# A work tile for each direction of the DeltaNet block inverses, and one decay buffer fewer

## The chip, the cores and the metric

The kernel runs on one core of one Trainium2 chip (trn2). The metric is the device time of one execution in microseconds (us), as the median of several runs. The core has five engines with a queue each: TensorE (PE in the profile, its weight loads PEld), VectorE (DVE), ScalarE (ACT), GpSimd (POOL) and SyncE (SP), which here only issues DMA transfers. Every queue is worked off in the order in which it was written.

## The reference

Two encoder layers on a (1, 1024, 1024) input. Layer 0 mixes tokens by softmax attention, layer 1 by a bidirectional gated DeltaNet; each is followed by a gated MLP with a short convolution. What matters here is the DeltaNet scan. Per direction and per chunk of 64 tokens it needs the inverse of a unit lower triangular matrix:

```
gc = cumsum(g); decay = exp(where(incl, gc[c] - gc[s], -inf))
L = (k*beta) @ k^T * decay * strict
sol = triangular_solve(L + I, [v*beta, k*beta*exp(gc)])      # u, w
attn = q @ k^T * decay
step:  v_new = u - w @ state;  o = q*exp(gc) @ state + attn @ v_new
       state = state*exp(gc_last) + k_dec^T @ v_new
```

The backward direction runs the same on the flipped sequence. There are 16 value heads on 8 key heads.

## The kernel before

All large products are float32 values split into two float32r parts (`split`, L108: an ACT cast to `hi`, a DVE subtraction to `lo`), and three matmuls of 128x512 for each pair of blocks (`dense`, L126, matmul at L134). They are the bulk of PE's work, here called the dense matmuls.

In the DeltaNet stage (`gdn`, L771) a loop runs over eight key heads j. Each pass emits the input projections of the next key head (`gdn_in`, L452: six products of 48 dense matmuls, a five-tap convolution on DVE at L448, silu on ACT at L449, and the results put into a DRAM tensor `pk`), and then, for the directions d = 0 and 1 of head j, `decay`, `inverse` and `chain`, and last `head_out`. A direction holds sixteen 128x128 blocks (eight double chunks, two value heads).

- `decay` (L539) builds the decayed blocks in four groups of four. Each group takes a tile `pr` from a ring of eight buffers, loads rows of cumulated gates into it from DRAM (`grow`, L549, an SP queue DMA), adds bias and mask (L551, DVE), takes exp (L553, ACT), makes `at` (L558), turns `pr` into the decayed q·k block (L559), and splits `at` into two float16 tiles `ah` (L561) and `al` (L562).
- `inverse` (L583) inverts all sixteen blocks together in a float16 tile `t0` and its transpose `w0`. It first clears with POOL those off-diagonal blocks of `t0` that the other direction filled (two memsets at L601, one at L602), writes the 32x32 diagonal blocks from `ah` (L606, DVE), multiplies with a mask into `w0` (L607, DVE), and starts on PE with products with an identity (L593, output `ip`, input `id`). Four levels of doubling follow, each PE to ACT or DVE and back, then the off-diagonal blocks (L640 to L664) and one refinement step (L672 to L681), which reads `t0` and `w0` to the end.
- `chain` (L685) steps through eight chunks. Step t loads `c` from `pk`, and reads the `pr` tile of group t // 2 as weights in its last matmul (L738). A `pr` buffer is free when the second step that uses it has passed L738.

`t0` and `w0` exist once and serve both directions of all heads. The order within each queue is made by a scheduler before the run, from priorities: `decay` and `inverse` are emitted inside `ahead(4)`, `chain` inside `ahead(2)`, so that they go before the dense matmuls of `gdn_in` where they are ready, and the dense matmuls fill what is left. When the last `gdn_in` is through, the output projection begins (L809): `split_rows` loads the finished heads' rows (`t<-od`) and splits them into `base` and `y` tiles, and dense matmuls with them follow. This place is called the seam below.

Of the kernel before, what the change touches and what calls it, by code (L numbers as in the profile page):

```python
# [9 lines left out]
F32 = mybir.dt.float32  # L10
F32R = mybir.dt.float32r
F16 = mybir.dt.float16
# [6 lines left out]
P = 128  # L19
# [18 lines left out]
def flat(t):  # L38
    return t.rearrange("p a b -> p (a b)")


class Trunk:
# [327 lines left out]
    def gates(self, ys, dp, tmp):  # L370


        nc, ap = self.nc, self.ap
# [12 lines left out]
        every = lambda t: t.rearrange("p (j v) -> p j v", v=2).unsqueeze(2).broadcast_to([P, 8, NC, 2])  # L386
        dtb = self.load("dtb", [P, 2, 16], dp, ap["gdn_dt"].partition_broadcast(P))
        alog = self.load("alog", [P, 2, 16], dp, ap["gdn_alog"].partition_broadcast(P))
        tri = dp.tile([P, 4, P], F32, name="pr", bufs=8)[:, :2]
        nc.sync.dma_start(out=tri, in_=ap["tri"])  # L390
        nc.scalar.activation(out=alog, in_=alog, func=AF.Exp)
        nc.vector.tensor_scalar(out=flat(alog), in0=flat(alog), scalar1=-1.0, scalar2=None, op0=ALU.mult)
# [8 lines left out]
        t = [flat(work()) for _ in range(4)]  # L401
# [137 lines left out]
    def decay(self, j, d, kks, qks, dp):  # L539


        nc = self.nc
        ah, al, prs = {}, {}, {}
        for i in (range(4) if d == 0 else range(3, -1, -1)):
            if i // 2 not in ah:
                ah[i // 2], al[i // 2] = (dp.tile([P, 8, P], F16, name=n, bufs=3) for n in ("ah", "al"))
            pr = prs[i] = dp.tile([P, 4, P], F32, name="pr", bufs=8)
            m0 = 16 * j + 4 * i
            nc.sync.dma_start(out=pr, in_=self.grow[d, m0:m0 + 4].partition_broadcast(P))  # L549
            for m in range(4):  # L550
                nc.vector.scalar_tensor_tensor(out=pr[:, m], in0=pr[:, m], in1=self.maskneg[:, d],  # L551
                                               scalar=self.ebias[:, d, m0 + m:m0 + m + 1], op0=ALU.add, op1=ALU.add)
            nc.scalar.activation(out=pr, in_=pr, func=AF.Exp)  # L553
            prn = pr.rearrange("p (n v) c -> p n v c", v=2)
            bc = lambda t: (t[i // 2][:, (i % 2) * 256:(i % 2) * 256 + 256].rearrange("p (n c) -> p n c", n=2)
                            .unsqueeze(2).broadcast_to([P, 2, 2, P]))
            at = dp.tile([P, 4, P], F32, name="at", bufs=1)
            nc.vector.tensor_tensor(out=at.rearrange("p (n v) c -> p n v c", v=2), in0=prn, in1=bc(kks), op=ALU.mult)  # L558
            nc.vector.tensor_tensor(out=prn, in0=prn, in1=bc(qks), op=ALU.mult)  # L559
            hi, lo = (t[i // 2][:, 4 * (i % 2):4 * (i % 2) + 4] for t in (ah, al))  # L560
            nc.scalar.copy(out=hi, in_=at)  # L561
            nc.vector.tensor_tensor(out=lo, in0=at, in1=hi, op=ALU.subtract)  # L562
        return ah, al, prs

    def delta_buffers(self, dp):
        nc = self.nc
        self.t0, self.w0 = (dp.tile([P, 16, P], F16, name=n, bufs=1) for n in ("t0", "w0"))
        nc.gpsimd.memset(self.t0, 0.0)
        self.maskneg = self.load("maskneg", [P, 2, P], dp)
        self.negoff = self.load("negoff", [P, P], dp)  # L570
        self.lvl = self.load("lvl", [P, 2, 4, 32], dp)
        self.cw5 = self.load("gdn_cw", [P, 32, 6], dp)
        self.o_gain = self.load("gdn_gain", [P, 1], dp)
        half = {}
        for n, w in (("mask2", P), ("id32", 32)):
            t = self.load(n, [P, w], dp)
            half[n] = dp.tile([P, w], F16, name=n + "_16", bufs=1)
            nc.vector.tensor_copy(out=half[n], in_=t)
        self.mask2, self.id32 = half["mask2"], half["id32"]
        self.nident16 = dp.tile([P, P], F16, name="nident16", bufs=1)  # L580
        nc.vector.tensor_scalar(out=self.nident16, in0=self.ident, scalar1=-1.0, scalar2=None, op0=ALU.mult)

    def inverse(self, d, ah, al, dp):  # L583
# [1 line left out]


        nc = self.nc
        t0, w0 = self.t0, self.w0
        up = [(Q32[i], Q32[i + 1]) for i in (0, 2)]
        dn = [(Q32[i + 1], Q32[i]) for i in (0, 2)]  # L590
        a, b = (slice(0, 64), slice(64, 128)) if d == 0 else (slice(64, 128), slice(0, 64))
# [5 lines left out]
        small = lambda n: dp.tile([P, 16, 32], F16, name=n, bufs=2 if n == "tp" else 1)  # L597


        for r, c in (up if d == 0 else dn):  # L600
            nc.gpsimd.memset(t0[r, :, c], 0.0)  # L601
        nc.gpsimd.memset(t0[a, :, b], 0.0)  # L602
        for h in ah:
            hs = slice(8 * h, 8 * h + 8)
            for q in Q32:
# [61 lines left out]
        for h in (range(4) if d == 0 else range(3, -1, -1)):  # L667
# [7 lines left out]
            r = dp.tile([P, 4, P], F16, name="r", bufs=2)  # L675
# [716 lines left out]
```

## Time and profile before

| what | value |
| --- | --- |
| median of 3 runs | 3449.74 us (3447.62 to 3450.36) |
| time of the profiled execution | 3439.26 us |
| its span, first to last instruction | 3437.5 us |
| mean granted TensorE clock | 0.981 of full speed |

The profiled execution is a run of its own, with the hardware profiler on. Its span lies 1.8 us below its own time, and its time 10.5 us below the median. Busy times and waits below are from it. A row's "idle before" is time in which the engine had nothing running, with the instruction that ended it; a wait on an engine that isn't the bound costs nothing.

### The profile page before, as it was taken

How to read it: one execution, taken by the hardware profiler on the slowest of the kernel's cores; microseconds unless marked ns; L12 is line 12 of the kernel's file. 1: busy time of each engine (PE TensorE's matmuls, PEld its weight loads, DVE VectorE, ACT ScalarE, POOL GpSimd, SP SyncE). 2: the span in 40 equal slices, each digit the busy share in tenths (PEclk: the TensorE clock that was granted, in tenths of full speed). 3: DMA queues.
4: the chain of work that ended last, by engine and by line, in shares of the span. 5: the costliest groups of instructions: out<-in, count | busy, mean ns of one | idle time of the engine just before them, and what ended most of it. 6: DMA issues, size and time to landing. Idle time of an engine off the chain costs nothing. (4 is left out here: it accounts for less than half of the span.)

```text
span 3437.5 us, 54135 instructions
## 1 busy us (share of the span) xinstructions
PE 3247.3 (94%) x19690; PEld 2620.0 (76%) x19690; DVE 2495.2 (73%) x4235; ACT 1741.5 (51%) x3224; POOL 842.4 (25%) x919
## 2 busy tenths in 40 slices
PE   7999999899999998899999999999898989999998
PEld 6877788677777876677777777777676867777786
DVE  5335886887776875778778787877853787777695
ACT  4235664544454454565555556666532544544453
POOL 1111330444442002121221212222120144444100
PEclk9999999999999999999999999999999999999999
DMA  3331006333324642332342424334356623332743
GB/s 127 104 113 59 32 31 191 122 106 111 112 94 168 218 129 65 102 111 88 113 126 81 136 92 130 102 113 132 102 175 206 204 98 110 101 105 92 244 132 109
DMA packets 249802, 411.20 MB, mean 120 GB/s; under 512 B 25536, under 2 KB 76096, under 8 KB 249536
## 3 DMA queue, kind: packets, MB, share of 16 engines
q1 hardware_dynamic: 249536, 407.76, 36.6%
q8 instruction: 155, 2.54, 0.3%
q14 instruction: 111, 0.91, 0.1%
HBM read 294.80 MB, written 107.61 MB: 117 GB/s over the span
## 5 line engine op out<-in xcount | busy, mean ns | idle before, releaser
L134 PE MATMUL mm<-base,wh 128*128 128x512 f32 x1248 | 480.1, 412 | 10.0 <-ACT base L109 5.9
L109 ACT CAST wh<-w_raw 128x512 fp32r<-128x512 f32 x275 | 169.9, 619 | 296.7 <-PE mm L134 175.6
L110 DVE TENSOR_TENSOR wl<-w_raw,wh 128x512 fp32r<-128x512 f32 x275 | 193.2, 707 | 138.2 <-ACT wh L109 137.1
L134 PE MATMUL mm<-yh,wh 128*128 128x512 f32 x736 | 282.6, 413 | 5.3 <-ACT t L291 2.7
L134 PE MATMUL mm<-yh,wl 128*128 128x512 f32 x736 | 280.6, 410 | 1.0 <-DVE wl L110 1.0
L134 PE MATMUL mm<-yl,wh 128*128 128x512 f32 x736 | 279.3, 408 | 0.3 <-POOL yl L110 0.2
L134 PEld LDWEIGHTS mm<-base,wh 128*128 128x128 f32 x1248 | 238.3, 191 | 49.6 <-ACT base L109 6.3
L153 POOL TENSOR_TENSOR rs<-rs,power 128x8 f32<-128x8 f32 (+2 forms) x38 | 63.8, 1679 | 824.8 <-DVE rs L152 824.7
L134 PE MATMUL mm<-base,wl 128*128 128x512 f32 x624 | 257.3, 412 | 6.4 <-DVE wl L110 6.4
L703 POOL TENSOR_SCALAR kd<-c,yds 128x128 f32<-128x128 f32 x224 | 95.2, 437 | 635.0 <-PE cp L732 444.8
L109 ACT CAST wh<-a 128x512 fp32r<-128x512 f32 x164 | 101.8, 622 | 256.7 <-PE mm L134 122.6
L109 ACT CAST wh<-s 128x512 fp32r<-128x512 f32 x212 | 131.4, 620 | 183.6 <-PE sp L134 87.3
L134 PE MATMUL sp<-base,wh 128*128 128x512 f32 (+1 forms) x672 | 211.5, 372 | 12.6 <-ACT wh L109 12.6
L448 DVE SCALAR_TENSOR_TENSOR t<-mm,gdn_cw,t 128x1023 f32<-128x1023 f32 (+1 forms) x128 | 163.1, 1276 | 6.8 <-ACT t L445 6.1
L134 PEld LDWEIGHTS mm<-yh,wh 128*128 128x128 f32 x736 | 140.6, 193 | 29.3 <-ACT t L291 3.6
L134 PEld LDWEIGHTS mm<-yl,wh 128*128 128x128 f32 x736 | 140.8, 192 | 27.8 <-POOL yl L110 1.6
L134 PEld LDWEIGHTS mm<-yh,wl 128*128 128x128 f32 x736 | 140.8, 191 | 26.5 <-DVE wl L110 1.7
L134 PE MATMUL sp<-base,wl 128*128 128x512 f32 (+1 forms) x432 | 157.7, 365 | 1.4 <-DVE wl L110 0.9
L134 PEld LDWEIGHTS sp<-base,wh 128*128 128x128 f32 x672 | 127.7, 190 | 34.3 <-ACT wh L109 13.0
L110 DVE TENSOR_TENSOR wl<-s,wh 128x512 fp32r<-128x512 f32 x170 | 142.0, 836 | 12.3 <-ACT wh L109 12.2
L978 POOL TENSOR_TENSOR s<-a,a 128x512 f32<-128x512 f32 x80 | 108.5, 1356 | 159.0 <-DVE s L978 106.0
L134 PEld LDWEIGHTS mm<-base,wl 128*128 128x128 f32 x624 | 119.1, 191 | 27.2 <-DVE wl L110 7.2
(522 smaller groups left out, 9362.4 us busy)
## 6 DMA issues: line engine op xcount, KB each, us to landing
a<-in_ffn_up_dram SPq DMA_DIRECT2D x160, 256.0 KB, 2.8
c<-pk SPq DMA_DIRECT2D x128, 320.0 KB, 3.1
w_raw<-in_gdn_in_dram SPq DMA_DIRECT2D x100, 256.0 KB, 2.8
g_t<-t SPq DMA_DIRECT2D x88, 256.0 KB, 2.0
raw<-g_t SPq DMA_DIRECT2D x88, 256.0 KB, 2.6
w_raw<-in_gdn_out_dram SPq DMA_DIRECT2D x68, 256.0 KB, 3.6
g<-t SPq DMA_DIRECT2D x66, 256.0 KB, 2.1
raw<-g SPq DMA_DIRECT2D x66, 256.0 KB, 2.8
```

Of the source, the lines that this page charges most:

```text
L109: self.nc.scalar.copy(out=hi, in_=src)
L110: (engine or self.nc.vector).tensor_tensor(out=lo, in0=src, in1=hi.bitcast(F32), op=ALU.subtract)
L134: self.nc.tensor.matmul(acc if one else acc[:, hs], lhsT=a, rhs=y[:, hs], start=(first and not onto and k + t == 0), stop=(last and k == n ...
L153: nc.gpsimd.tensor_tensor(out=r, in0=v, in1=self.power[:, :w], op=ALU.pow)
L448: nc.vector.scalar_tensor_tensor(out=o, in0=a, scalar=c[:, i:i + 1], in1=o, op0=ALU.mult, op1=ALU.add)
L703: nc.gpsimd.tensor_scalar(out=kd[:, e], in0=kn, scalar1=col(self.yds, e), scalar2=1.0, op0=ALU.mult, op1=ALU.mult)
L978: e.tensor_tensor(out=s[i], in0=x, in1=z, op=op)
```

## The change

`t0` becomes a list of two tiles, one for each direction, both cleared in full at the start. `w0` stays one tile (the list holds it twice). Each inverse clears now the blocks that it itself filled in the head before, in its own tile, since nothing else writes there. The number and sizes of these clears stay as they were; one full memset is added at the start. The ring `pr` has seven buffers in place of eight; its first allocation, `tri` in `gates`, is from the same ring.

```diff
-        tri = dp.tile([P, 4, P], F32, name="pr", bufs=8)[:, :2]
+        tri = dp.tile([P, 4, P], F32, name="pr", bufs=7)[:, :2]
...
-            pr = prs[i] = dp.tile([P, 4, P], F32, name="pr", bufs=8)
+            pr = prs[i] = dp.tile([P, 4, P], F32, name="pr", bufs=7)
...
-        self.t0, self.w0 = (dp.tile([P, 16, P], F16, name=n, bufs=1) for n in ("t0", "w0"))
-        nc.gpsimd.memset(self.t0, 0.0)
+        self.t0 = [dp.tile([P, 16, P], F16, name=f"t{d}", bufs=1) for d in range(2)]
+        self.w0 = 2 * [dp.tile([P, 16, P], F16, name="w0", bufs=1)]
+        for t in self.t0:
+            nc.gpsimd.memset(t, 0.0)
...
-        t0, w0 = self.t0, self.w0
+        t0, w0 = self.t0[d], self.w0[d]
...
-        for r, c in (up if d == 0 else dn):
+        for r, c in (dn if d == 0 else up):
             nc.gpsimd.memset(t0[r, :, c], 0.0)
-        nc.gpsimd.memset(t0[a, :, b], 0.0)
+        nc.gpsimd.memset(t0[b, :, a], 0.0)
```

With eight buffers, each `pr` of a direction takes over the buffer that the same group of the same direction had one head earlier. With seven, the first three groups take over buffers of groups two to four of that direction one head earlier, and the fourth takes over the buffer of the first group of the direction just before it: the inverse of (j, 1) can't be begun in full before the chain of (j, 0) has passed its second step, and that of (j, 0) not before the chain of (j-1, 1) has.

The scheduler puts all queues of the DeltaNet stage in another order; outside of it a few rows of the second MLP move. Three places follow. The lines after the change are three higher from L571 on.

The queue of SP around head 5 (`pk5`), with tile numbers. Before: the last two `pr` loads of (5, 1) stand among the stores of head 5's `v` rows, ahead of the first loads of its chain (`c`).

```order
L549 DMA pr_23433<-grow_11848 128x512
L468 DMA pk5_20202<-h_20651 128x4x128
L549 DMA pr_23445<-grow_11848 128x512
L468 DMA pk5_20202<-h_20659 128x4x128
L121 DMA w_raw_22252<-in_gdn_in_dram 128x512
L121 DMA w_raw_22435<-in_gdn_in_dram 128x512
L121 DMA w_raw_22441<-in_gdn_in_dram 128x512
L468 DMA pk5_20202<-h_20735 128x4x128
L468 DMA pk5_20202<-h_20743 128x4x128
L121 DMA w_raw_22500<-in_gdn_in_dram 128x512
L698 DMA c_23208<-pk5_20202 128x640
L698 DMA c_23225<-pk5_20202 128x640
```

After: the fourth of them (`pr_23447`) stands behind four `c` loads of the chain of (5, 0).

```order
L701 DMA c_23210<-pk5_20204 128x640
L701 DMA c_23227<-pk5_20204 128x640
L771 DMA od8_22097<-z_22124 128x512
L121 DMA w_raw_22508<-in_gdn_in_dram 128x512
L701 DMA c_23254<-pk5_20204 128x640
L766 DMA z_22133<-zd9_18602 128x512
L701 DMA c_23281<-pk5_20204 128x640
L771 DMA od9_22098<-z_22133 128x512
L549 DMA pr_23447<-grow_11850 128x512
```

So this load moved from before the chain of (5, 0) to behind its second step.

The queue of DVE at the same inverse, from the fourth group's first operation to the mask product that ends the preparation. Before:

```order
L551 SCALAR_TENSOR_TENSOR pr<-pr,ebias,maskneg 128x128 x4
L558 TENSOR_TENSOR at<-pr,kks 128x512
L559 TENSOR_TENSOR pr<-pr,qks 128x512
L448 SCALAR_TENSOR_TENSOR t<-mm,gdn_cw,t 128x1022
L562 TENSOR_TENSOR al<-at,ah 128x512
L606 TENSOR_TENSOR t_11705<-ah,id_16_11724 32x8x32 x4
L448 SCALAR_TENSOR_TENSOR t<-mm,gdn_cw,t 128x1023
L607 TENSOR_TENSOR w_11706<-t_11705,mask_16_11720 128x1024
```

After, with chain steps 2 and 3 of (5, 0) in between (`st`, `o`, `r`):

```order
L551 SCALAR_TENSOR_TENSOR pr<-pr,ebias,maskneg 128x128 x4
L739 TENSOR_TENSOR st<-cp,sd 128x256
L745 TENSOR_TENSOR o<-cp,o 128x256
L770 SCALAR_TENSOR_TENSOR z<-sp,gdn_gain,z 128x512
L717 SCALAR_TENSOR_TENSOR r_23291<-cp,negc,c 128x128 x2
L558 TENSOR_TENSOR at<-pr,kks 128x512
L559 TENSOR_TENSOR pr<-pr,qks 128x512
L448 SCALAR_TENSOR_TENSOR t<-mm,gdn_cw,t 128x1022
L562 TENSOR_TENSOR al<-at,ah 128x512
L609 TENSOR_TENSOR t_11706<-ah,id_16_11726 32x8x32 x4
L739 TENSOR_TENSOR st<-cp,sd 128x256
L610 TENSOR_TENSOR w_11707<-t_11706,mask_16_11722 128x1024
```

One convolution row (L448) left the piece, and rows of the chain came in.

The queue of PE at the seam. Before, two dense matmuls of the output projection (`base_27581`, `yh`) are followed at once by the last inverse:

```order
L134 MATMUL mm<-base_11450,wl 128x512
L134 MATMUL mm<-yh,wl 128x512
L134 MATMUL mm<-base_27581,wh 128x512
L134 MATMUL mm<-yh,wh 128x512
L593 LDWEIGHTS w_11706
L593 MATMUL ip<-id_16_11724,w_11706 128x32
```

After, what follows the first two (with a refinement step of the inverse before in between) is dense matmuls on one row of `base` after the other, two products side by side:

```order
L134 MATMUL mm<-base_27583,wh 128x512 x2
L134 MATMUL mm<-yl,wh 128x512
L134 MATMUL mm<-base_27583,wl 128x512
L134 MATMUL mm<-yh,wl 128x512
L531 MATMUL sp<-ident,t 128x128 x4
L134 MATMUL mm<-yl,wh 128x512
L134 MATMUL mm<-base_27583,wl 128x512
L134 MATMUL mm<-yh,wl 128x512
L531 MATMUL sp<-ident,t 128x128 x4
L134 MATMUL mm<-base_27586,wh 128x512 x2
```

The last inverse moved from 2 to 71 dense matmuls behind the seam, and the eight rows of `base` are taken one after the other without it in between.

## Rows read from the trace of the kernel before

**Rows 1.** The page: span, and busy time, share and instructions of each engine.
```profile
span 3437.5 us, 54135 instructions
PE 3247.3 (94%) x19690; PEld 2620.0 (76%) x19690; DVE 2495.2 (73%) x4235; ACT 1741.5 (51%) x3224; POOL 842.4 (25%) x919
```
**Rows 2.** Windows, DeltaNet loop: length, busy time by engine, clock, DMA share, GB/s.
```profile
1400.00:2480.00 1080.00, 1015.50 (x9058) 806.56 (x9057) 859.05 (x1913) 636.57 (x1384) 227.94 (x436) 0.98 0.34 107
```
**Rows 3.** Waits of PE, 1400 to 2480: total us, times, longest.
```profile
PE ip L593 <- DVE w L607: 11.7, 20, 1.7
PE ip L593 <- DVE w L622: 8.3, 7, 1.5
...
PE mm L134 <- ACT base L109: 5.9, 1, 5.9
```
**Rows 4.** Windows, one pass of the loop, same columns as rows 2.
```profile
2038.83:2184.37 145.54, 138.57 (x1232) 111.16 (x1233) 116.89 (x263) 88.94 (x193) 31.88 (x62) 1.00 0.36 113
```
**Rows 5.** The clear at L602: who waited for it (us, times).
```profile
  POOL kd L703: 12.8, 5
  DVE st L736: 2.1, 1
  DVE w L607: 0.3, 1
```
**Rows 6.** Timeline, POOL and DVE, one inverse of direction 0 (start, us, what).
```profile
2083.15 0.95 POOL L602 MEMSET t<- 64x1024 f16 x1
...
2116.65 0.27 DVE L606 TENSOR_TENSOR t<-ah,id 32x256 f16<-32x256 f16 x1
```
**Rows 7.** Timeline, all engines, before the inverse of (5, 1).
```profile
2170.59 0.71 PE L738 MATMUL cp<-y,pr 128*128 128x128 f32 x4
2171.34 0.32 SPq L549 DMA_DIRECT2D pr<-grow  x1
2174.94 1.14 DVE L551 SCALAR_TENSOR_TENSOR pr<-pr,ebias,maskneg 128x128 f32<-128x128 f32 x4 [2.39 <-DMA pr<-grow]
2178.11 0.69 DVE L558 TENSOR_TENSOR at<-pr,kks 128x512 f32<-128x512 f32 x1 [2.02 <-ACT pr L553]
...
2182.73 0.39 PE L134 MATMUL mm<-yl,wh 128*128 128x512 f32 x1
2183.63 0.68 DVE L607 TENSOR_TENSOR w<-t,mask 128x1024 f16<-128x1024 f16 x1
2184.37 0.56 PE L593 MATMUL ip<-id,w 128*128 128x32 f16 x16 [1.25 <-DVE w L607]
```
**Rows 8.** Lines, chain steps and output transposes on PE: count, busy us, mean ns, idle.
```profile
L726 PE MATMUL cp<-r,w 128*128 128x128 f32 x448 | 84.9, 292 | 4.7 <-DVE r L714 4.6
L738 PE MATMUL cp<-y,pr 128*128 128x128 f32 x512 | 84.2, 285 | 0.3
...
L710 PE MATMUL cp<-st,c 128*128 128x256 f32 x224 | 72.5, 405 | 1.9 <-DVE st L736 1.8
...
L766 PE MATMUL sp<-ident,o 128*128 128x128 f32 x128 | 23.1, 282 | 4.2 <-DVE o L760 3.2 <-DVE z L767 0.9
```
**Rows 9.** Timeline, PE, an inverse of direction 0: its start.
```profile
2267.35 0.36 PE L593 MATMUL ip<-id,w 128*128 128x32 f16 x8 [0.49 <-DVE w L607]
```
**Rows 10.** Timeline, PE, the first inverse: waits late in it.
```profile
1420.59 0.57 PE L593 MATMUL ip<-x,w 128*128 128x32 f16 x16 [1.54 <-DVE w L622]
...
1432.18 0.21 PE L661 MATMUL ip<-x,w 64*64 64x64 f16 x1 [0.67 <-ACT x L658]
```
**Rows 11.** Timeline, SP, ACT and PE at the seam.
```profile
2464.77 17.94 SPq L831 DMA_DIRECT2D t<-od  x3
2471.53 0.60 ACT L109 CAST base<-t 128x512 fp32r<-128x512 f32 x1
2472.18 0.80 PE L134 MATMUL mm<-base,wh 128*128 128x512 f32 x1 [5.87 <-ACT base L109]
...
2475.21 0.61 PE L593 MATMUL ip<-id,w 128*128 128x32 f16 x16 [1.71 <-DVE w L607]
```

## The prediction

> **What bounds the kernel now.** I read the page first. TensorE is busy 3247.3 of 3437.5 us, 94% [rows 1]: it is the bound, and a change counts only by what it does to PE's idle time or to its number of instructions, and this one adds no instruction to PE. The reader is to see that only some 190 us of idle time exist in the whole kernel. Then I read the windows of the DeltaNet loop, 1400 to 2480 us, the one place where the edited code runs: PE is busy 1015.5 of 1080.0 us, 64.5 idle, and DVE follows at 80% [rows 2]. One pass for one key head takes 145.54 us with 138.57 busy, so 7 idle [rows 4]. No gain here can exceed 64.5 us, and it would have to come from waits that the two edits touch. So the waits of PE in the loop came next: the waits for `w` at L607, the last step of preparing an inverse, are 11.7 us in 20 waits, 0.6 each, spread over sixteen inverses; the last of them, 1.71 us, belongs to the seam [rows 3, 11], which leaves 10.0 for fifteen. Then there is one wait of 5.9 us on `base` at the seam [rows 3, 11]. The other waits in the loop belong to PE's way through an inverse or to weight splits, and the change doesn't alter what those depend on.
>
> **The second tile.** It takes away one dependence: the clears of `t0` and the diagonal blocks had to follow the last refinement step of the inverse before. Does anything wait there? In an inverse of direction 0 the last clear began at 2083.15 and took 0.95 us, and the first diagonal block was written at 2116.65 [rows 6]: the tile had been ready for 32.6 us. The waiters on that clear say the same for the whole run: `w` at L607 waited 0.3 us for it, once; `st` 2.1 us, once; POOL's own `kd` 12.8 us in five waits [rows 5], and POOL is busy 227.94 of 1080 us [rows 2] and PE isn't among the waiters. So the direct gain is 0.3 us at most, and I take 0. The work that hides the clears is the rest of the pass; without that cover they would cost 1 to 3 us per inverse (0.95 for the one at L602, at most as much for each of the two at L601). The added memset at the start clears one more tile while POOL has nothing else; 0. `w0` stays single, so `w` at L607 must still follow the refinement before.
>
> **The seventh buffer.** This is the edit that can cost. Rows 7 show the path from a freed buffer to a start, before the inverse of (5, 1): L738 ends at 2171.30 (2170.59 + 0.71), the load is issued at 2171.34, L551 starts at 2174.94 when it has landed, L558 at 2178.11 after exp, L607 ends at 2184.31, and PE starts at 2184.37 [rows 7]. That is 13.0 us. PE has 52 dense matmuls to do meanwhile, until 2183.12, so 0.227 us each, and then idles 1.25 us. With seven buffers the same load waits for the second chain step of (5, 0), and the scheduler has put the inverse later for it. Between that step's last L738 and the start of the inverse of (5, 1) stand now 22 dense matmuls (5.0 us), 8 transposes at L766 (23.1/128 = 0.18 each, 1.4), 6 products at L710 and L711, 4 at L726, 4 at L732 and 4 at L738. The program has half as many of these as the profile has records, so a product costs twice the busy time of a record: 72.5/224 x 2 = 0.65, 84.9/448 x 2 = 0.38, 84.2/512 x 2 = 0.33 [rows 8]; I price L711 as L710 and L732 as L738. Together 3.9 + 1.5 + 1.3 + 1.3, so the cover is 14.4 us. For the other inverses of direction 1 the same count gives 12.7 to 14.4, 13.8 in the mean, against 52 dense matmuls or 11.8 us in (4, 1), (5, 1) and (6, 1) before. The path changes by one convolution row less (L448, about 1.1 us if it costs as much as L551's four pieces, 1.14) and by chain rows of DVE (`st`, `o`, `z`, two `r`) that are put between L551 and L558, where DVE waited 2.02 us for exp anyway [rows 7]. If these fit, the path is about 12 and the wait goes; if they don't, it is 13 to 15.7 (the five rows at 0.4 to 0.7 each, the durations of L558 and L607, come to 2.7). What is queued behind on DVE is the next chain step, and PE's rows of chain steps 4 and 5 stand in that same cover, so a late `pr` also holds up the chain. The 10.0 us of waits at L607 I share evenly between the directions, 5 each: single waits of direction 1 are longer, 1.25 against 0.49 [rows 7, 9], those of direction 0 more. I take half of the first 5 back, **-2.5 us**, between -5 and +8.3 (path 15.7, wait 1.9, seven times 13.3, less the 5).
>
> In direction 0 the fourth load waits in the same way for the direction before, but only the second half of the inverse needs it. Its cover is 11.5 to 15.3 us by the same prices, and the first half is ready sooner than now, where PE waits 0.49 [rows 9]. I take **-1.5 us** over eight inverses, between -5 and +4 (three with a cover of 11.5 and a path of 13.0).
>
> The Trainium skill, page Perfetto Trace Analysis, section Optimization Strategy, says that the same gap coming back on the engine that should be saturated can mean too little SBUF for the next tile, a buffer count too small. The L607 wait before each inverse is such a gap, its releaser leads back to a freed `pr` buffer [rows 7], and by that rule taking a buffer away goes the wrong way: it speaks for the slower rival below.
>
> **The order.** The scheduler puts the inverses at other distances. Counted in dense matmuls, starts stood some 140 apart; now from (j, 0) to (j, 1) it is about 200 and from there to (j+1, 0) about 97. The chains stay about where they were; the last one ends 59 dense matmuls later, which 166 dense matmuls (38 us) still cover before the rows of the last head are needed: 0. The first inverse is denser with waits: before its last level product and L640 it loses four dense matmuls (0.9) and eight transposes (1.4 at L766's price), at most 2.3, where PE already waited 1.54; before L657 and L661 it gains some, at most 0.9 [rows 10]. I take **+1.4**.
>
> At the seam PE waited 5.87 us for `base`, whose load was issued at 2464.77, behind the last `pr` and `pk` rows on SP, and then 1.71 for the last inverse [rows 11]. Now the first of these loads stands ahead of the last `pr` load, and the last inverse begins 71 dense matmuls behind the seam. So up to 7.6 us can go. On the other side nothing fills PE now while eight rows of `base` come in one after the other, with 12 dense matmuls (2.7 us) for each, and one load too late costs what it cost before, 5.9. I take **-3**, nearer to the gain because the one late row had been late by its place on SP.
>
> **Sum.** 0 - 2.5 - 1.5 + 1.4 - 3 = -5.6 us. The profiled execution took 3439.26 us (span 3437.5), so it would be 3433.7; the median of the runs is 3449.74, 10.5 above it, and the difference carries over: 3444.1 us. Its own range, from the four terms' ends taken as not all on one side, is 3437 to 3453.
>
> **Rivals.** A: all waits that the edits reach vanish: the 10.0 at L607, the 7.6 at the seam, with 1.4 lost in the first inverse, so -16.2 and 3433.5 us. For it: the cover of 13.8 against a path of 12. Against: the chain's rows now stand in both queues there, and no wait in a loop so near to full (94%) goes without another showing up. B, the other side: the fourth `pr` load is exposed. Path 15.7 against a cover of 13.8 gives +8.3 in direction 1, +4 in direction 0, +1.4 in the first inverse, -3 at the seam: +10.7, about 3460 us. It decides (over 0.2%) from a path of some 15.3 us on, when direction 1 waits 1.5 us each. For it: before, three inverses of direction 1 waited about 1.2 us with 11.8 cover, and DVE, 80% busy, now has chain rows in the way. C: the seam starves, one more 5.9 where I take -3, nothing gained elsewhere: +7.3 and 3457 us. D: nothing comes of it, since the clears never bound and the scheduler hides the buffer: 3449.7 us.
>
> **How the numbers follow.** Some 0.2% (6.9 us) is what a measurement of this kernel can tell from no change, so "the same" is 3442.8 to 3456.6. My forecast gets 0.48, A 0.25, B 0.15, C 0.06, D 0.06. The forecast's range reaches over the bound on the fast side: of its 0.48 I give 0.12 to faster, 0.33 to the same and 0.03 to slower; with A faster is 0.37; with D and a part of C (0.02) the same is 0.41; slower is 0.03 + 0.15 + 0.04 = 0.22. The range 3432 to 3462 takes in A and B as computed and leaves one in five outside, most of it for reorderings that none of these sums holds.
>
> **What the changed profile would show.** PE's waits on L607 in the loop (now L610): 6 us or less if I am right, near 0 for A, 17 or more for B, with DVE's L551 waiting for the `pr` load and that load issued right after the second chain step's L738. The clears at L605 far ahead of the diagonal blocks, as before: if PE's time improves while they were never waited for, the tile wasn't the cause. At the seam one wait on `base` under 3 us, and no wait for L607 in front of it; for C several. The forecast is wrong if the pass between two inverses of one direction differs from 145.5 us by over 1 us, since that alone makes 8 us.

## The result, and the profile after

| | before | after |
| --- | --- | --- |
| median, runs of the first comparison | 3450.05 us (4 runs) | 3431.42 us (4 runs) |
| ratio | | 0.9949, 95% interval [0.9932, 0.9966] |
| profiled execution, span | 3437.5 us | 3427.4 us |
| mean granted clock of the profiled execution | 0.981 | 0.986 |

The change made the kernel 18.6 us faster. The forecast was 5.6 us; its sign is right and its size is a third. 3431.42 lies 0.6 us under the low end of the range; from the forecast's own base the ratio gives 3449.74 x 0.9949 = 3432.1, just inside it. It is rival A's time (3433.5) that came nearest. One later run of the kernel before was slow (4511 us at a mean granted clock of 0.652) and is left out of all that follows.

The page of the changed kernel, its first lines, against [rows 1]:

```profile
span 3427.4 us, 54083 instructions
PE 3232.4 (94%) x19690; PEld 2608.5 (76%) x19690; DVE 2495.7 (73%) x4235; ACT 1731.8 (51%) x3222; POOL 858.0 (25%) x920
```

PE runs the same 19690 matmuls but is busy 14.9 us less, and the span is 10.1 us shorter: outside its busy time PE has not gained, it has lost 4.8 us. The same matmuls in less busy time point to a higher clock while they run. Second profiles agree: PE is busy 3245.4 us in the kernel before (run e8 below) and 3233.5 in the changed one (e1).

The waits of PE in the DeltaNet loop, 1400 to 2480 us, against [rows 3] (total us, times, longest):

```profile
PE cp L713 <- DVE st L739: 10.6, 12, 1.8
PE cp L729 <- DMA c<-pk: 6.0, 6, 2.0
PE sp L513 <- DVE kks L515: 5.7, 4, 1.8
PE mm L134 <- DVE t L448: 5.1, 3, 4.1
PE cp L729 <- DVE r L717: 4.5, 6, 2.2
PE ip L596 <- DVE w L625: 4.4, 6, 2.2
...
PE ip L596 <- DVE w L610: 1.1, 2, 0.6
```

The reader is to see two things. The wait for the mask product, 11.7 us in 20 waits before (L607), is 1.1 us in two (L610). And in its place stand waits of the chain: 10.6 us for `st` (1.8 before) and 6.0 us for the loads of `c` (1.2 before). The loop as a whole has lost hardly any idle time. Its windows, against [rows 2] (length, busy time of PE, PEld, DVE, ACT, POOL, clock, DMA share, GB/s):

```profile
1400.00:2480.00 1080.00, 1017.80 (x9033) 809.23 (x9031) 857.46 (x1909) 627.64 (x1383) 236.07 (x434) 0.99 0.36 109
```

64.5 us of idle time before, 62.2 after.

The path to the inverse of (5, 1) in the changed kernel, which answers to [rows 7]: timeline, PE, SP and DVE from the L741 that frees the buffer.

```profile
2195.24 0.61 PE L741 MATMUL cp<-y,pr 128*128 128x128 f32 x4
...
2195.88 0.32 SPq L549 DMA_DIRECT2D pr<-grow  x1
...
2199.36 1.17 DVE L551 SCALAR_TENSOR_TENSOR pr<-pr,ebias,maskneg 128x128 f32<-128x128 f32 x4 [1.56 <-DMA pr<-grow]
2200.46 0.41 DVE L739 TENSOR_TENSOR st<-cp,sd 128x256 f32<-128x256 f32 x1
2200.79 0.41 DVE L745 TENSOR_TENSOR o<-cp,o 128x256 f32<-128x256 f32 x1
2201.12 0.73 DVE L770 SCALAR_TENSOR_TENSOR z<-sp,gdn_gain,z 128x512 f32<-128x512 f32 x1
2202.09 0.61 DVE L717 SCALAR_TENSOR_TENSOR r<-cp,negc,c 128x128 f32<-128x128 f32 x2 [0.24 <-PE cp L714]
2202.62 0.68 DVE L558 TENSOR_TENSOR at<-pr,kks 128x512 f32<-128x512 f32 x1
...
2207.44 0.68 DVE L610 TENSOR_TENSOR w<-t,mask 128x1024 f16<-128x1024 f16 x1
...
2208.54 0.56 PE L596 MATMUL ip<-id,w 128*128 128x32 f16 x16
```

The buffer is free at 2195.85, the mask product is done at 2208.12: 12.3 us. The chain's five rows on DVE (2200.46 to 2202.70) lie in the time in which DVE would wait for exp, and PE's row at 2208.54 carries no wait.

The clears, which answer to [rows 6]: timeline, POOL and DVE, the inverse of (5, 0).

```profile
2108.05 0.95 POOL L605 MEMSET t<- 64x1024 f16 x1
...
2113.68 0.27 DVE L609 TENSOR_TENSOR t<-ah,id 32x256 f16<-32x256 f16 x1
```

The tile is ready 4.7 us before its first diagonal block is written. It was 32.6 us before the change; either way nothing on PE waits for it. With one tile and seven buffers (run e2 below) it is 4.8 us at the same inverse, so it is the ring and not the second tile that moved the clears.

The seam, 10 us windows with the columns above, of the kernel before and then of the changed kernel:

```profile
2465.00:2475.00 10.00, 2.63 (x8) 1.33 (x6) 7.09 (x14) 7.13 (x16) 0.00 (x0) 0.82 0.41 145
2475.00:2485.00 10.00, 8.04 (x109) 6.11 (x110) 9.29 (x20) 4.68 (x6) 1.95 (x1) 0.50 0.16 49
2485.00:2495.00 10.00, 6.67 (x77) 5.15 (x76) 9.28 (x24) 4.28 (x8) 0.99 (x2) 0.84 0.74 253
2495.00:2505.00 10.00, 10.00 (x124) 7.77 (x125) 6.95 (x14) 7.39 (x15) 1.42 (x4) 0.82 0.72 232
```

```profile
2450.00:2460.00 10.00, 7.60 (x63) 6.06 (x62) 9.82 (x20) 7.12 (x12) 0.00 (x0) 1.00 0.04 9
2460.00:2470.00 10.00, 5.17 (x26) 3.18 (x26) 7.86 (x16) 6.53 (x9) 1.33 (x1) 0.84 0.50 150
2470.00:2480.00 10.00, 9.48 (x40) 6.69 (x38) 6.16 (x12) 6.18 (x24) 2.39 (x2) 0.82 0.75 229
2480.00:2490.00 10.00, 8.55 (x48) 6.91 (x49) 6.76 (x13) 5.47 (x13) 6.05 (x11) 1.00 0.77 276
```

Before, PE was busy 2.6 of 10 us and then ran at the lower of its two clock levels (0.50, 1.2 GHz), came back, had the gaps of the last inverse, and fell once more: (0.18 + 0.50 + 0.16 + 0.18) x 10 = 10.2 us lost to the clock. After, there is one fall, 3.4 us. In the first inverse it is the same in small: 1400 to 1450 had a clock of 0.83 and has 0.90, 8.5 against 5.0 us lost (second profiles: 0.86 and 0.90).

### The profile page after: what moved, and what is told of

Its sections match the earlier page's. It is cut to its first block, busy times and chain, and to the rows that moved or that the text cites. A ratio compares the mean times of both kernels' runs of the same rounds, so it can differ in the third digit from the quotient of the medians.

```text
span 3427.4 us, 54083 instructions
## 1 busy us (share of the span) xinstructions
PE 3232.4 (94%) x19690; PEld 2608.5 (76%) x19690; DVE 2495.7 (73%) x4235; ACT 1731.8 (51%) x3222; POOL 858.0 (25%) x920
## 5 line engine op out<-in xcount | busy, mean ns | idle before, releaser
L134 PE MATMUL mm<-base,wh 128*128 128x512 f32 x1248 | 474.4, 408 | 10.1 <-DVE t L448 9.2
L134 PE MATMUL sp<-base,wh 128*128 128x512 f32 (+1 forms) x672 | 212.1, 373 | 16.1 <-ACT wh L109 16.1
L448 DVE SCALAR_TENSOR_TENSOR t<-mm,gdn_cw,t 128x1023 f32<-128x1023 f32 (+1 forms) x128 | 162.9, 1275 | 4.4 <-ACT t L445 4.1
L134 PEld LDWEIGHTS mm<-yh,wl 128*128 128x128 f32 x736 | 139.8, 190 | 25.6 <-DVE wl L110 1.7
L110 DVE TENSOR_TENSOR wl<-s,wh 128x512 fp32r<-128x512 f32 x170 | 141.9, 835 | 11.2 <-ACT wh L109 11.1
L109 ACT CAST gh<-raw 128x512 fp32r<-128x512 f32 x132 | 81.7, 619 | 121.1 <-DMA raw<-g_t 65.6
```

Of the source, the lines that this page charges most:

```text
L109: self.nc.scalar.copy(out=hi, in_=src)
L110: (engine or self.nc.vector).tensor_tensor(out=lo, in0=src, in1=hi.bitcast(F32), op=ALU.subtract)
L134: self.nc.tensor.matmul(acc if one else acc[:, hs], lhsT=a, rhs=y[:, hs], start=(first and not onto and k + t == 0), stop=(last and k == n ...
L448: nc.vector.scalar_tensor_tensor(out=o, in0=a, scalar=c[:, i:i + 1], in1=o, op0=ALU.mult, op1=ALU.add)
```

## The experiments

Each was compared with the kernel before on one chip (59 runs of it in three comparisons, medians 3444.4, 3445.0 and 3444.6 us; the row "after" is the first comparison). "Distances" are dense matmuls from the start of the inverse of (j, 0) to that of (j, 1), and from there to (j+1, 0), means without the steps inside the first and the last head. The last three columns are worked out from the PE timeline of the profiled execution, between the 4480th and the 6900th dense matmul, which hold the whole loop and the seam: the time, PE's idle time in it, and the time lost to the clock (one minus the granted clock, times the time, in 10 us windows).

| run | tiles, ring | distances | last inverse behind the seam | ratio, interval | time | idle | clock |
| --- | --- | --- | --- | --- | --- | --- | --- |
| before | 1, 8 | 135, 151 | 2 | 1 | 1226.6 | 73.5 | 25.6 |
| e8, before again | 1, 8 | 135, 151 | 2 | one run, 3439.13 us | 1230.4 | 78.0 | 22.2 |
| after | 2, 7 | 200, 93 | 71 | 0.9949 [0.9932, 0.9966] | 1214.8 | 69.1 | 13.6 |
| e1, after again | 2, 7 | 200, 93 | 71 | 0.9948 [0.9932, 0.9965] | 1212.8 | 68.2 | 11.9 |
| e2 | 1, 7 | 197, 98 | 76 | 0.9950 [0.9931, 0.9968] | 1212.6 | 61.8 | 18.7 |
| e3 | 2, 8 | 150, 139 | 3 | 0.9979 [0.9966, 0.9991] | 1225.5 | 77.7 | 18.8 |
| e4, control of e3 | 1, 8 | 135, 151 | 2 | 1.0002 [0.9989, 1.0015] | 1227.3 | 76.0 | 20.5 |
| e5 | 1, 8, last held back | 124, 161 | 73 | 0.9974 [0.9964, 0.9984] | 1216.1 | 65.3 | 13.6 |
| e6 | 1, 7, last let go | 197, 98 | 3 | 0.9956 [0.9941, 0.9970] | 1218.2 | 67.3 | 20.5 |
| e7 | 1, 6 | 195, 96 | 79 | 1.0068 [1.0052, 1.0085] | 1258.8 | 90.9 | 29.0 |
| e9 | 1, 8, a priority | 119, 167 | 1 | 1.0027 [1.0015, 1.0040] | 1239.1 | 83.3 | 20.6 |
| e10 | 1, 9 | 106, 176 | 0 | 1.0028 [1.0019, 1.0036] | 1239.6 | 82.9 | 22.1 |
| e11 | 2, 6 | 194, 92 | 89 | 1.0078 [1.0063, 1.0093] | 1261.6 | 88.3 | 30.7 |
| e12 | 1, 5 | 171, 119 | 115 | 1.0117 [1.0101, 1.0132] | 1268.4 | 86.8 | 61.9 |

Two profiles of one kernel differ by up to 4.5 us in a column (the first four rows), so smaller differences between rows say nothing.

My theory after the first result was C: the order that the ring of seven makes keeps PE's clock up. The rivals were W (waits alone), T (the second tile), and then, between parts of the order, S (the seam) against L (the distances in the loop), and R (any other order moves the time).

**e1, the changed kernel again.** No edit.

> The changed kernel once more, against the kernel before on one chip. Theory W (waits): the gain is idle time of PE that the two edits took away, so both runs differ by what the two profiles differ in idle time, under 2 us, and the rest was drift between chips: ratio 0.997 to 1.000. Theory C (clock): the new order keeps PE from falling to its lower clock level at the seam and in the first inverse; the first profiles show 11 us less of it, so the ratio is 0.994 to 0.997 again, and this profile again shows less time at the lower level at the seam than the kernel before.

Measured: 3425.63 against 3444.4 us, 0.9948. The gain is real and no drift between chips, so W's "drift" falls. As for C, the six runs showed a mean clock of 0.9847 and the 59 of before 0.9814. Within a kernel, a run whose clock was 0.001 higher was 2.3 us shorter (a line through all runs of this study, one intercept for each kernel), so by this estimate 0.0033 is worth some 8 of the 19 us. The rest is at equal clock. C is under half of it.

**e2, the ring alone.**

```diff
-            pr = prs[i] = dp.tile([P, 4, P], F32, name="pr", bufs=8)
+            pr = prs[i] = dp.tile([P, 4, P], F32, name="pr", bufs=7)
```

(The same for `tri`.)

> Only the ring of seven decay buffers; one t0 tile for both directions, cleared as before. The order on PE has inverses 203 and 99 dense matmuls apart, as the changed kernel has (202 and 97), and the last inverse 76 dense matmuls behind the seam (71). Theory C (the order that the ring makes carries the gain): as fast as the changed kernel within 0.2%, ratio 0.993 to 0.997. Theory T (the second tile carries it): the ratio is 1.000 or above, since the clears must follow the last inverse and the ring only costs. If both parts are needed: in between.

Measured: 0.9950. One tile and seven buffers are as fast as two tiles and seven. The part of the change that I had taken for its risk carries the whole gain. But its profile shows the gain in another form. Its page:

```profile
span 3428.2 us, 54095 instructions
PE 3246.0 (95%) x19690; PEld 2616.2 (76%) x19690; DVE 2493.7 (73%) x4235; ACT 1735.5 (51%) x3222; POOL 845.2 (25%) x919
```

PE is busy as long as before (3246.0 against 3247.3 us); what fell is its idle time, 182.2 against 190.2 us, which is W's cause, though more than the 2 us that W had. (e6 below has 3247.1 busy and 182.1 idle.) And its clock falls at the seam too, 8.0 us lost in these 20 us (10.2 before):

```profile
2460.00:2470.00 10.00, 5.30 (x20) 2.65 (x18) 9.66 (x16) 7.80 (x27) 3.63 (x4) 0.50 0.40 119
2470.00:2480.00 10.00, 9.56 (x34) 6.87 (x35) 6.61 (x13) 5.16 (x8) 1.95 (x1) 0.70 0.61 184
```

So the clock that the changed kernel's profiles gain there isn't what makes a ring of seven fast, and C falls as the common cause. By the estimate under e1, the clock of e2's timed runs (0.9832) is worth some 4 of its 17 us. In the table, idle time and clock loss together come to 99 and 100 us in the two profiles of before, and to 80 to 83 us in after, e1 and e2: much the same gain, split differently, and no run shows what decides the split.

**e3 and e4, the tile alone, and its control.** e3 is the changed kernel with eight buffers; both load four constants through a `pr` buffer and keep them in float16 (two are shown), with the junk output of the squares:

```diff
-        self.negoff = self.load("negoff", [P, P], dp)
-        self.lvl = self.load("lvl", [P, 2, 4, 32], dp)
+        self.negoff = narrow("negoff", P)
+        self.lvl = narrow("lvl", 2 * P).rearrange("p (a b c) -> p a b c", a=2, b=4)
...
-                sq = dp.tile([P, P], F32, name="sq", bufs=1)
+                sq = dp.tile([P, P], F16, name="sq", bufs=1)
```

> Only the second t0 tile; the ring keeps eight buffers. To find the 1.6 KB, four constants are held in float16 and loaded through the ring, and the junk output of the squares is float16. The order on PE stays evenly spaced (about 144 dense matmuls), the last inverse begins 3 dense matmuls behind the seam. Theory T: as fast as the changed kernel or faster, ratio 0.990 to 0.996. Theory C: no gain, ratio 0.998 to 1.002, and PE at its lower clock level at the seam for some 10 us of lost time, as in the kernel before.

> The kernel before with only the space savings of the two-tiles, eight-buffers run (float16 constants, float16 junk of squares), no second tile. The order on PE is that of the kernel before. Every theory expects a ratio of 0.999 to 1.001; what it differs by is taken off the two-tiles run.

Measured: 0.9979 and 1.0002. The tile alone gives 7 us, neither theory's number. Its order isn't that of before (150 and 139), so this is the tile or the order; e9 shows that an order alone moves the time as much, there to the slower side. With the ring of seven the tile adds nothing (e1, e2), with six nothing (e7 and e11, intervals that overlap).

**e5 and e6, the seam against the loop.** In e5 the fourth group of (7, 1) shares a buffer of its own with the first of (7, 0), and has to wait for the chain; in e6, with a ring of seven, it doesn't have to wait.

```diff
+            one = j == 7 and i == 0
+            pr = prs[i] = dp.tile([P, 4, P], F32, name="prl" if one else "pr", bufs=1 if one else 8)
```

```diff
+            last = j == 7 and d == 1 and i == 0
+            pr = prs[i] = dp.tile([P, 4, P], F32, name="prl" if last else "pr", bufs=1 if last else 7)
```

> The kernel before with its ring of eight, but the last inverse, that of (7, 1), is held back: its fourth decay group gets a buffer of its own that it shares only with the first group of (7, 0), so it must wait for the second chain step of (7, 0), as in the changed kernel. All other inverses keep a spacing near the even one (117 to 178 dense matmuls, 142 in the mean), and the last begins 73 dense matmuls behind the seam in place of 2. Theory S (seam): PE's fall to its lower clock and its waits around the seam are the gain, so this alone gives most of it, ratio 0.995 to 0.997. Theory L (loop): the spacing of 200 and 97 lets PE wait less inside the loop, so this gives little, ratio 0.998 to 1.000. If both carry half: 0.997 to 0.998.

> The mirror of it: one t0 tile and the ring of seven, in the order of the run with the ring alone (inverses 200 and 99 dense matmuls apart), but the fourth decay group of the last inverse has a buffer of its own, so that this inverse begins 3 dense matmuls behind the seam, as in the kernel before. Theory S: the gain is gone, ratio 0.998 to 1.000, and PE waits some 6 us for base and falls to the lower clock twice at the seam. Theory L: the gain stays, ratio 0.995 to 0.997, with the waits for the mask product (L607) in the loop under 3 us against 11.7 before. Both half: 0.997 to 0.998.

Measured: 0.9974 and 0.9956. The loop's order without the late last inverse keeps 0.0044 of the 0.0050, so S falls as the main cause: the late last inverse is worth what lies between 0.9956 and 0.9950, and that is less than the intervals. e6 isn't the seam of before in full: PE waited 2.2 us for `base` and not 6, then 5.2 for `t`, and lost 6.9 us to one fall of the clock from 2460 to 2480. With e2, which loses 8.0 there and keeps the gain, that is enough against the seam. e5 doesn't show the seam alone, as its loop too was ordered anew (124 and 161), and its profile is of the fastest of its twelve runs. The waits of e6 in the loop and at the seam, 1385 to 2610 us:

```profile
PE ip L673 <- DVE w L682: 7.5, 7, 2.8
PE mm L134 <- DVE t L448: 6.8, 2, 5.2
PE cp L711 <- DVE st L737: 6.7, 10, 1.2
PE sp L767 <- DVE z L768: 5.8, 6, 1.9
PE sp L513 <- DVE kks L515: 3.8, 4, 1.6
PE ip L594 <- DVE w L608: 3.7, 5, 1.3
```

Here too the mask product (L608) fell, to 3.7 us, and the chain's `st` rose. What counts is the net, and windows of the loop's middle show it best: before, the changed kernel, e6, and e2, PE's instructions in the same 1000 us.

```profile
1450.00:2450.00 1000.00, 952.23 (x8464) 758.26 (x8464) 792.11 (x1786) 594.37 (x1307) 225.15 (x431) 0.99 0.35 111
```

```profile
1450.00:2450.00 1000.00, 955.04 (x8487) 763.09 (x8487) 793.92 (x1790) 585.13 (x1306) 230.43 (x430) 0.99 0.37 111
```

```profile
1450.00:2450.00 1000.00, 959.26 (x8504) 765.30 (x8503) 794.24 (x1794) 587.50 (x1306) 225.60 (x432) 0.99 0.36 110
```

```profile
1450.00:2450.00 1000.00, 960.28 (x8532) 765.40 (x8532) 796.38 (x1797) 589.47 (x1309) 225.06 (x432) 1.00 0.36 111
```

With seven buffers PE is busy 3 to 8 us more in the same time, and gets 23 to 68 more instructions through. The three profiles of the order of before (with e8 and e4) have 8410 to 8464 of them, and the four with seven buffers (with e1) 8486 to 8532.

**e7, e11 and e12, still fewer buffers.** Only the number of buffers: 6, 6 with two tiles, 5.

> One t0 tile and a ring of six. The order is that of seven in kind: inverses about 195 and 95 dense matmuls apart, the last 79 behind the seam. If it is the order that the shorter ring makes, and not the number of free buffers, this is about as fast as seven, ratio 0.994 to 0.997. If a shorter ring costs (rival B of the prediction, a decay load exposed), PE waits for the mask product or the chain again and the ratio is 0.999 or more.

> Two t0 tiles and a ring of six. With one tile a ring of six had the ratio 1.0068. If the second tile is worth something where inverses follow each other closely (here 86 to 101 dense matmuls apart), this comes out lower by 0.003 or more. If the tile is worth nothing, as the clears' early ends say: 1.005 to 1.009.

> One t0 tile and a ring of five, so that no direction can begin more than one group ahead of the chain before it. Inverses 171 and 117 dense matmuls apart, the last chain ends 132 dense matmuls later than before, so the cover behind it shrinks from 60 to 29 us. Rival B, the exposed load: slower than six, 1.01 to 1.03. If six was slow for its order and not for the load: between 0.995 and 1.007.

Measured: 1.0068, 1.0078 and 1.0117. One buffer below seven, the distances are nearly the same and the kernel is 23 us slower than the kernel before by the ratio, and 40 slower than with seven. e7's timeline at the inverse of (5, 0), PE and SP, shows why:

```profile
2130.90 0.36 PE L593 MATMUL ip<-id,w 128*128 128x32 f16 x8 [0.26 <-DVE w L607]
...
2133.43 0.61 PE L738 MATMUL cp<-y,pr 128*128 128x128 f32 x4
...
2134.07 0.32 SPq L549 DMA_DIRECT2D pr<-grow  x1
...
2142.44 0.69 PE L738 MATMUL cp<-y,pr 128*128 128x128 f32 x4
...
2143.16 0.32 SPq L549 DMA_DIRECT2D pr<-grow  x1
...
2153.52 0.36 PE L593 MATMUL ip<-id,w 128*128 128x32 f16 x8
```

Two groups now wait for the chain, each a load that is issued within 0.1 us of the L738 that frees its buffer. The second half of the inverse starts 22.6 us behind the first; with seven it was 6.3 (2120.49 and 2126.75 in the changed kernel). The wait on L607 is small all the same, 0.26, since the scheduler had put other rows of PE ahead of the second half: an exposed load shows up as work moved, and then as waits of the chain. The waits of e7, same stretch:

```profile
PE cp L710 <- DVE st L736: 17.2, 17, 2.6
PE cp L726 <- DVE r L714: 8.0, 11, 1.7
```

With five, the loop's clock falls as well, 61.9 us lost. So rival B is a real mechanism, and it begins between seven and six buffers: 40 us are far more than the 9 that e9's order moved, though no run has the order of six with more buffers.

**e9 and e10, another order with the same buffers, and a ring of nine.**

```diff
-        with self.ahead(2, 1100):
+        with self.ahead(2, 1300):
```

> The kernel before with its one tile and its ring of eight; only a number among the scheduler's priorities differs (1100 to 1300 for the head of the next input projection). The order of the whole stage comes out another: inverses about 120 and 170 dense matmuls apart in the last heads (from (j, 0) to (j, 1) the shorter of the two, the reverse of the ring of seven), the last 1 dense matmul behind the seam. Theory R (any other order of this stage moves the time, whatever the buffers): off 1 by 0.003 or more to either side. Theory L (the long distance from (j, 0) to (j, 1), which the ring of seven forces, is what helps): no gain, 0.999 or above. A ratio of 0.995 would say that the ring has nothing to do with it but through the luck of the order.

> One t0 tile and a ring of nine, more than the kernel before. Inverses about 102 and 185 dense matmuls apart, the last at the seam. Theory B (buffers help, as the rule on repeated gaps has it): faster than with eight, 0.997 or below. Theory L: the long distance is on the other side, so no gain, 0.999 or above. Theory R: anything from 0.995 to 1.005.

Measured: 1.0027 and 1.0028. More buffers aren't faster. The Trainium skill, page Perfetto Trace Analysis, section Optimization Strategy, says that a repeated gap can mean too few buffers, as the prediction cites it. By that, nine would have been expected to beat eight, and here it didn't. And a number in the scheduler that touches no buffer moves the time by 9 us, so R holds, though 0.0027 is a little under the 0.003 that it named. Both are slower with (j, 1) close behind (j, 0), as L says; but e5, with nearly the distances of e9, is faster than before. That isn't its seam alone: from 1450 to 2450 us PE gets 8505 instructions through in e5 and 8258 in e9. So the distances alone don't decide, and L stands only for what the ring of seven makes of the order, not for a rule about distances.

**e8, the kernel before again.**

> The kernel before once more, for a second profile. Every theory expects 3434 to 3454 us, about 74 us of PE idle time between the start of the first inverse and the first dense matmuls behind the last head, two falls to the lower clock at the seam, and one in the first inverse.

Measured: 3439.13 us, 78.0 us idle (73.5 in the first profile), with two falls at the seam again. The difference of 4.5 us is what two profiles of one kernel can show.

## Why the prediction was right or wrong

The sign was right, and the second tile was rightly taken for nothing. The size wasn't right, and where the time came near rival A, that is partly luck. Step by step:

- **The second tile, taken as 0.** Right where it was tested: nothing with seven buffers (0.9948 with, 0.9950 without) or with six. At eight it came with 7 us that the runs can't tell from the order.
- **The seventh buffer at direction 1, -2.5, and direction 0, -1.5.** This is the term that was too small. The path I had put at "about 12" was 12.3; the chain's rows did fit into exp's time. But I took only half of the waits back, and they went almost wholly: 11.7 to 1.1 us, which was rival A. The load is issued right behind the chain's L741, as I had named for B, and yet PE doesn't wait for it.
- **That a wait which goes is gained.** This premise of the sum, and of rival A, failed too, as the prediction's own argument against A had it (no wait goes without another showing up). In the same 1080 us PE's idle time fell by 2.3 us only, since waits on `st` (1.8 to 10.6) and `c` (1.2 to 6.0) grew. Between the same dense matmuls it fell by 4 to 10 us (69.1 and 68.2 against 73.5 and 78.0), and by 12 to 16 in e2. Rival A thus came near the time by luck in part: its 16.2 us of idle time didn't go.
- **The clock, left out of the sum.** The prediction's first premise, that a change counts only by PE's idle time or its number of instructions, is wrong: the changed kernel's PE is busy 14.9 us less with the same 19690 matmuls. The clock loss in the loop and at the seam is 12 to 14 us against 20 to 26, and over the timed runs the clock is worth some 8 us by the estimate under e1. I had rows with the granted clock and summed only waits, though at the seam the wait was followed by matmuls at half speed (the windows of 0.82 and 0.50).
- **The 10.5 us from the profiled execution to the median, carried over.** They didn't carry over: after the change the distance is 2.2 us. Between the profiled executions the forecast was -5.6 and the result -10.1 us; the other 8.5 of the 13.0 us that the forecast was short by are here. One execution is one draw: the 59 runs of before lie between 3434 and 3454 us.
- **The seam, -3.** The wait on `base` went from 5.87 us to 0.6, its first load being issued at 2443.61 in place of 2464.77; a wait of 4.1 us on `t` (L448) took its place. By e2 and e6 the seam is worth little.
- **The first inverse, +1.4.** About right for what it counted, idle time: from 1400 to 1450 us it is 7.7 and 7.9 us in the two profiles of before, 9.5 and 8.4 after. The clock there, which it left out, gave 2 to 3.5 us back.
- **The tail, 0.** Behind the seam the sum missed something: PE's one wait for `wh` where the next stage begins grew from 12.6 to 16.1 us (11.2 and 16.0 in the second profiles), so some 4 us are given back there. The late last inverse isn't shown to be the reason, since e2, where it is as late, has 13.0.
- **Rival B.** Not at seven, but at six: +23 us where I had +10.7.
- **The sign of being wrong, a pass other than 145.5 us.** It can't decide: passes between two inverses of one direction ran from 134 to 160 us before and from 123 to 154 after, and the one that the figure is from took 145.0.

What stays open: the profiled executions differ by 10 to 12 us (3439.26 and 3439.13 before, 3429.2 and 3427.2 after), the medians by 19. The profiled executions of before lie 6 to 11 us under its medians, those of after 2.2 us under and 1.6 above, and no trace shows these microseconds. Which property of the order makes the loop better is open as well. The runs show that it is the ring of seven, and not the tile, the seam or the distances alone. That the ring works through the order is argued: at one and the same order a buffer less can only add a wait, but no run has the order of seven with eight buffers. All the orders with seven that ran are close relatives, so whether seven is more than a lucky order for this kernel is open too.

## What to carry to other kernels

Where a scheduler makes the order, a buffer count is also a constraint on that order, and the order can be worth more than the wait that the buffer removes: time the counts on both sides (here nine, eight, seven and six gave 1.0028, 1, 0.9950, 1.0068) and each part of a change alone. A gap on the bound engine is to be priced with the clock behind it, and what carries a gain is to be read from more than one run that has it: here two runs of the same speed showed it as clock in one and as idle time in the other. And with orders, differences of 0.3% say little about the edit: a priority that touched nothing else moved as much.

## What was unexpected of the hardware

The profiles show PE at two clock levels only, and the time at the lower one moves with the order of the work: at the seam it follows a stretch in which PE was busy 2.6 of 10 us, and with five buffers it costs 61.9 us in the loop although PE's idle time there, 86.8 us, is less than with six (90.9). So idle time alone doesn't say what the clock will cost.
